# Projections of a two-layer attention and expert kernel on pairs of scaled 16-bit floats

## The chip, the cores and the metric

The kernel runs on one core of one Trainium2 chip. The metric is the device time of one execution in microseconds. The time given for a kernel is the median of several executions; the profile is of one further execution, whose own time is given beside its span.

## The reference

The reference is the trunk of a small encoder on x of 256 frames by 1024. Layer 0 mixes the frames by latent attention: x is projected to ranks (384 for queries, 256 for keys and values, 64 for a rotary key), the ranks are normalised, and then projected up to 8 heads. Layer 1 mixes them by attention over the 64 keys that a small indexer picks. Behind each mixer stands a layer of experts (PEER): a query picks, for each of 8 heads, the 16 best pairs of keys out of 128 x 128, that is 16 of 16384 experts. An expert is a row of w_down and a row of w_up.

```python
def _peer(x, w_q, sub_keys, w_down, w_up):
    q = (xt @ w_q).reshape(T, PEER_HEADS, 2, PEER_QDIM // 2)
    ...
    u = w_down[e_blk]
    a = jnp.einsum('td,ted->te', x_blk, u).astype(jnp.float32)
    hg = (jax.nn.gelu(a, approximate=False) * g_blk).astype(w_up.dtype)
    return jnp.einsum('te,ted->td', hg, w_up[e_blk]).astype(x_blk.dtype)

def reference(...):
    for i in range(DEPTH):
        m = _mla_mixer(...) if i % 2 == 0 else _dsa_mixer(...)
        x = _layernorm(DN_ALPHA * x + m, ln_gain[i, 0], ln_bias[i, 0])
        f = _peer(x, ...)
        x = _layernorm(DN_ALPHA * x + f, ln_gain[i, 1], ln_bias[i, 1])
    return x
```

The weights are normal with a spread of 1/32 for the projections from 1024, x is normal with spread 1, and the gains of the rank norms are about 8. Everything is in 32-bit floats.

## The kernel before, in words

The kernel doesn't gather experts (256 frames of 128 choices make 32768 choices of 16384 experts); it multiplies x by all 16384 down rows (product d, 128 blocks of 128 experts), applies the gelu, multiplies by a gate matrix that is zero where an expert was not chosen (built with the small product G from one-hot matrices), and multiplies by all up rows (product y). The array A in the arena holds gates and activations, 128 blocks by 256 frames.

Every projection works on pairs. A 32-bit operand is split in two: the high part is the value rounded to the type float32r by a copy on ScalarE, the low part is the value minus the high part, by VectorE. A product is three matmuls into one PSUM bank: high by high, high by low, low by high (`mm3`, `proj`, `rows`, all through `mm` at L277). `proj` makes a transposed result, with the weights stationary and x moving in 256 columns (24 matmuls a block); `rows` has x stationary and moves the weights in 512 columns (12 matmuls a block).

The class `Stream` holds the order of all weight blocks of the kernel, 128 x 1024 each, 604 in all: four raw buffers that SyncE fills by DMA (L101), and two rings of four places for the high and the low parts. `get` hands out the parts of one block and first fills the stream: blocks are split three ahead of the one that is taken, and loaded three ahead of that. `_split` makes the high part on ScalarE (L119) and the low part on VectorE (L123), or on GpSimd (L121) for one block in four while `share` says so. `_place` puts blocks whose parts are stationary 16 elements further along in the ring than blocks whose parts are moving (SKEW). The x of a stage is split once, into xh and xl.

The stages follow one another on TensorE: `mla` (0 to 105 us of the trace), `peer(0)` (to 878), `dsa` (to 1018), `peer(1)` (to the end). At the passage between two stages, `finish` interleaves the end of one product, the layer norm of the first half of the frames, and the start of the next product; the order there is written out by hand.

In `peer`, while TensorE works on d, VectorE works on the choice of experts in the background: `choose` is a generator that gives the cost of each of its steps in ns (1210 for a list of the 16 best of 128, 1160 for one of the pairs, and so on), and `spend` lets it run for an income of PACE after each block. So VectorE's order is: low part of a block, PACE worth of the choice, low part of the next. When the choice is done, the gates are made: for each group of four frames `prepare` builds one-hot matrices on VectorE (L1119), GpSimd (L1121) and ScalarE (L1125), `place` multiplies them (G, 8 matmuls of 128 columns, 16-bit) and writes the group into A. Two groups are placed for each pair of blocks of d.

`Norm` is a layer norm with its sums on VectorE (L351, with a sum written out beside the result), its squares on ScalarE (L359) and its power on GpSimd (L371). `first` is the first projection: it takes x and the first block in pieces, with a few idle matmuls at the start; one of its low parts is on GpSimd (L1227). `attention` works head by head: scores, exponentials on ScalarE (L578), transposes, outputs, which `split_ps` splits (L304, L305) for the output projection. In `finish` of the last stage, the output leaves by the queues of SyncE and ScalarE (L437).

Of the kernel before, what the change touches and what calls it, by code (L numbers as in the profile page):

```python
# [18 lines left out]
P = 128  # L19
T = 256  # L20
# [22 lines left out]
PACE = 1450  # L43
# [6 lines left out]
SKEW = 16  # L50
DSA_POOL = 3
MAGIC = 12582912.0


class Stream:
# [5 lines left out]
    def __init__(self, nc, raw, hi, lo):  # L61
        self.nc, self.raw, self.hi, self.lo = nc, raw, hi, lo
        self.dve = self.act = lambda emit: emit()
        self.blocks, self.ready = [], []
        self.at = []
# [5 lines left out]
    def add(self, src, w=D, moving=False):  # L71
        for i in range(src.shape[0]):
            self.blocks.append((src[i], w))
            self.at.append(self._place(0 if moving else SKEW))

    def _place(self, skew):

        if not self.at:
            return skew
        slot = (self.at[-1] // D + 1) % RING  # L80
        if slot and self.at[-1] + self.blocks[len(self.at) - 1][1] > slot * D + skew:
            slot = (slot + 1) % RING
        return slot * D + skew

    def _clear(self, n, first):

        a, b = self.at[n], self.at[n] + self.blocks[n][1]
        return all(self.at[m] + self.blocks[m][1] <= a or b <= self.at[m] for m in range(first, n))

    def parts(self, i):  # L90
        at = self.at[i]
        return [ring[:, at : at + self.blocks[i][1]] for ring in (self.hi, self.lo)]

    def _load(self, upto):
        while self.n_loaded <= min(upto, len(self.blocks) - 1):
            src, w = self.blocks[self.n_loaded]
# [15 lines left out]
    def _split(self, upto, pooled, first):  # L112
        nc = self.nc
        while self.n_split <= min(upto, len(self.blocks) - 1) and self._clear(self.n_split, first):
            w = self.blocks[self.n_split][1]
            self._load(self.n_split)
            raw = self.tiles[self.n_split][:, :w]
            hi, lo = self.parts(self.n_split)
            self.act(lambda: nc.scalar.copy(hi, raw))  # L119
            if pooled or self.share and (self.n_split - 1) % self.share == 0:  # L120
                nc.gpsimd.tensor_tensor(lo, raw, hi.bitcast(F32), op=ALU.subtract)  # L121
# [1220 lines left out]
```

## Time and profile before

| what | value |
|---|---|
| median of 3 runs | 1797.89 us (1797.75 to 1798.05) |
| the profiled execution's time | 1797.2 us |
| its span in the trace | 1795.4 us |
| granted TensorE clock | 0.999 |
| busy: PE, PEld, DVE, ACT, POOL | 1784.0, 1631.1, 1336.2, 1053.2, 406.2 us |
| read from HBM | 329.16 MB |

PE is TensorE's matmuls, PEld its loads of stationary operands, DVE VectorE, ACT ScalarE, POOL GpSimd, SP SyncE. A row of a group gives the line of the kernel, the engine and operation, what is written from what, the shape (partitions by elements, and type), and the count; then the busy time in us and the mean in ns of one, and the engine's idle time before them with what ended it. Matmuls overlap, so the mean of one is a latency; what one costs in a stream is the distance from start to start. In a timeline a row begins with its start and its length in us. In the chain of the execution that ended last, a piece is a stretch in which one engine went from one instruction to the next without a wait.

### The profile page before, as it was taken

Reading aid. Unit: us, or ns where it says so; the run is one execution under the profiler, and the core shown is the slowest. Engines: PE = TensorE matmul, PEld = TensorE weight load, DVE = VectorE, ACT = ScalarE, POOL = GpSimd, SP = SyncE. Lnnn points to the kernel's source line nnn. Section 1 sums busy time; section 2 is a strip of 40 time slices with the busy share of each in tenths; the row PEclk is TensorE's granted clock in tenths of the full one; section 3 lists DMA queues with packets and bytes.
Section 4 is the critical chain, followed back from the end, with each engine's and each line's share of the span. In section 5 each row is a group of like instructions: output and inputs, shape, how many; then the busy total and the mean of one; then the engine's idle time right before and its main releaser. Section 6 shows DMA issues by size and latency. Waiting matters only on the chain.

```text
span 1795.4 us, 32370 instructions
## 1 busy us (share of the span) xinstructions
PE 1784.0 (99%) x12495; PEld 1631.1 (91%) x12495; DVE 1336.2 (74%) x2319; ACT 1053.2 (59%) x1832; POOL 406.2 (23%) x288
## 2 busy tenths in 40 slices
PE   9999999999999999999999999999999999999998
PEld 8899999999998888888889899999999988888886
DVE  6688998888985555555688789997889865555555
ACT  6655545888864444444467554557888754444443
POOL 2012354555520000000023013544555400000000
PEclk9999999999999999999999999999999999999999
DMA  6555556444556565655646455565454476565553
GB/s 233 211 175 179 189 200 194 159 165 165 165 188 222 190 198 191 196 191 196 205 164 225 172 173 185 192 200 177 165 164 162 157 246 197 190 197 190 196 191 118
DMA packets 93468, 335.47 MB, mean 187 GB/s; under 512 B 10368, under 2 KB 11392, under 8 KB 93312
## 3 DMA queue, kind: packets, MB, share of 16 engines
q1 hardware_dynamic: 93024, 332.87, 56.0%
q8 instruction: 98, 1.61, 0.3%
q14 instruction: 58, 0.48, 0.1%
q10 hardware_dynamic: 288, 0.52, 0.1%
HBM read 329.16 MB, written 4.19 MB: 186 GB/s over the span
## 4 chain that ended last, share of the span: by engine, by line
PE 98%; DVE 1%; issue 0%; DMA 0%; ACT 0%; POOL 0%; SPq 0%; DVEq 0%; POOLq 0%; ACTq 0%
PE y L277 41%; PE d L277 39%; PE pq L277 4%; PE G L277 3%; PE q L277 3%; PE v L277 1%; PE qw L277 1%; PE s L277 1%; PE ps L277 1%; PE h L277 1%; PE qi L277 1%; PE o L277 1%; PE qn L277 0%; DMA raw<-in_mla_h 0%; PE pt L280 0%
## 5 line engine op out<-in xcount | busy, mean ns | idle before, releaser
L123 DVE TENSOR_TENSOR lo<-raw,hi 128x1024 fp32r<-128x1024 f32 (+1 forms) x556 | 747.5, 1346 | 289.5 <-ACT hi L119 288.0
L119 ACT CAST hi<-raw 128x1024 fp32r<-128x1024 f32 (+1 forms) x583 | 611.0, 1049 | 522.8 <-PE d L277 222.4
L277 PE MATMUL d<-xh,hi 128*128 128x256 f32 x2048 | 572.9, 280 | 0.0
L277 PE MATMUL d<-xh,lo 128*128 128x256 f32 x2048 | 566.8, 277 | 0.0
L277 PE MATMUL d<-xl,hi 128*128 128x256 f32 x2048 | 566.8, 277 | 0.0
L277 PEld LDWEIGHTS d<-xh,lo 128*128 128x128 f32 x2048 | 385.2, 188 | 0.0
L277 PEld LDWEIGHTS d<-xh,hi 128*128 128x128 f32 x2048 | 384.9, 188 | 0.0
L277 PEld LDWEIGHTS d<-xl,hi 128*128 128x128 f32 x2048 | 384.7, 188 | 0.0
L277 PE MATMUL y<-hi,xh 128*128 128x512 f32 x1088 | 337.8, 390 | 0.0
L277 PE MATMUL y<-lo,xh 128*128 128x512 f32 x1088 | 337.7, 389 | 0.0
L277 PE MATMUL y<-hi,xl 128*128 128x512 f32 x1088 | 337.2, 389 | 0.0
L1121 POOL TENSOR_TENSOR gate<-hot,gate 128x512 f16<-128x512 f16 x128 | 220.5, 1741 | 214.4 <-DVE hot L1119 214.4
L277 PEld LDWEIGHTS y<-lo,xh 128*128 128x128 f32 x1088 | 204.1, 188 | 42.8 <-DVE lo L123 0.3
L277 PEld LDWEIGHTS y<-hi,xl 128*128 128x128 f32 x1088 | 204.2, 188 | 42.4
L277 PEld LDWEIGHTS y<-hi,xh 128*128 128x128 f32 x1088 | 203.8, 188 | 41.9
L371 POOL TENSOR_TENSOR st<-st,mhalf 128x1 f32<-128x1 f32 x8 | 4.4, 550 | 802.1 <-DVE st L369 802.1
L1125 ACT ACTIVATE gate<-hot,rest 128x128 f16<-128x128 f16 x512 | 165.9, 411 | 1.1 <-DVE hot L1119 1.0
L1182 ACT CAST xh<-arena 128x512 fp32r<-128x512 f32 x128 | 79.7, 623 | 145.5 <-PE y L277 145.3
L1183 DVE TENSOR_TENSOR xl<-arena,xh 128x512 fp32r<-128x512 f32 x128 | 88.2, 692 | 72.7 <-ACT xh L1182 72.7
L121 POOL TENSOR_TENSOR lo<-raw,hi 128x1024 fp32r<-128x1024 f32 x27 | 65.2, 2414 | 218.4 <-ACT hi L119 213.1
L1119 DVE TENSOR_TENSOR hot<-iota,place 128x1024 f16<-128x1024 f16 x128 | 85.7, 709 | 32.3 <-PE G L277 32.2
L1043 POOL TENSOR_TENSOR arena<-arena 128x800 f32<-128x800 f16 x32 | 71.0, 2229 | 58.1 <-DVE arena L1040 58.1
(220 smaller groups left out, 1803.5 us busy)
## 6 DMA issues: line engine op xcount, KB each, us to landing
raw<-in_down SPq DMA_DIRECT2D x256, 512.0 KB, 3.3
raw<-in_up SPq DMA_DIRECT2D x256, 512.0 KB, 4.3
raw<-in_peer_q SPq DMA_DIRECT2D x24, 512.0 KB, 4.2
raw<-in_dsa_qk SPq DMA_DIRECT2D x16, 512.0 KB, 3.4
raw<-in_mla_w_o SPq DMA_DIRECT2D x8, 512.0 KB, 5.6
arena<-in_peer_q SPq DMA_DIRECT2D x8, 512.0 KB, 5.1
raw<-in_dsa_v SPq DMA_DIRECT2D x8, 512.0 KB, 4.4
raw<-in_dsa_w_o SPq DMA_DIRECT2D x8, 512.0 KB, 4.3
```

Source lines behind the costliest of these rows:

```text
L119: self.act(lambda: nc.scalar.copy(hi, raw))
L121: nc.gpsimd.tensor_tensor(lo, raw, hi.bitcast(F32), op=ALU.subtract)
L123: self.dve(lambda: nc.vector.tensor_tensor(lo, raw, hi.bitcast(F32), op=ALU.subtract))
L277: return pe(lambda: nc.tensor.matmul(o, l, r, start=start, stop=stop, skip_group_check=True))
L371: nc.gpsimd.tensor_tensor(st[:, 5:6], st[:, 4:5], mhalf, op=ALU.pow)
L1043: nc.gpsimd.tensor_tensor(o.rearrange("p k c -> p c k"), same, cell[t][:, h, :, None].to_broadcast([P, CELLS, TOPK]), op=ALU.mult)
L1119: nc.vector.tensor_tensor(hot, iota4[:, None].to_broadcast([P, 2, P, 4]), place16[:, :, None, four].to_broadcast([P, 2, P, 4]), op=ALU.is_ ...
L1121: nc.gpsimd.tensor_tensor(gate[:, 0], hot[:, 1].rearrange("p c j -> p j c"), gate16[:, four, None].to_broadcast([P, 4, P]), op=ALU.mult)
L1125: nc.scalar.mul(gate[:, 1, j, :], hot[:, 1, :, j], rest[:, t : t + 1])
L1182: nc.scalar.copy(hh, a)
L1183: nc.vector.tensor_tensor(al, a, hh.bitcast(F32), op=ALU.subtract)
```

## The change

The pairs become 16-bit floats (F16), with the value first scaled by a power of two: x by 2^12, the weights by 2^17, the normalised ranks by 2^9 and their weights by 2^16, the attention's outputs by 2^10 and the output weights by 2^17, A by 2^13 and the up rows by 2^14. The high part is a scaled copy on ScalarE to 16 bits; the low part is one operation on VectorE, value times scale minus high part, written in 16 bits. That operation also writes the sum of the low parts of each partition into a column of its own of an array `sums`. The scale is taken out where a result leaves PSUM (`unscale`, a scaled copy in the place of the copy; the gelu's scale; the rope tables, scaled on the host; the epsilon of the norms).

```diff
+class Split:
+    def high(self, o, src, unit, engine="act"):
+        nc, unit = self.nc, unit if self.short else 1.0
+        if engine == "act":
+            return nc.scalar.copy(o, src) if unit == 1.0 else nc.scalar.mul(o, src, unit)
...
+    def low(self, o, src, unit, hi, total=None):
+        nc = self.nc
+        if not self.short:
+            return nc.vector.tensor_tensor(o, src, hi.bitcast(F32), op=ALU.subtract)
+        return nc.vector.scalar_tensor_tensor(o, src, unit, hi, op0=ALU.mult, op1=ALU.subtract, accum_out=total)
...
+    half = F16 if short else F32R
...
-    xh = wide.tile([P, NC, T], F32R, tag="xh", name="xh")
-    xl = wide.tile([P, NC, T], F32R, tag="xl", name="xl")
+    xh = wide.tile([P, NC, T], half, tag="xh", name="xh")
+    xl = wide.tile([P, NC, T], half, tag="xl", name="xl")
```

The rings of `Stream` become pools of four tiles each, without the offset of SKEW and without the places that skip a part of the ring. Where GpSimd makes the low part, ScalarE scales the raw block in place first, and sums the low part later, when the stream is two blocks on:

```diff
+    def _pooled(self, i):
+        nc, short = self.nc, self.split.short
+        _, w, unit = self.blocks[i]
+        self._load(i)
+        raw = self.tiles[i][:, :w]
+        if short:
+            self.act(lambda: nc.scalar.mul(raw, raw, unit))
+        hi, lo = self.parts(i)
+        self.act(lambda: nc.scalar.copy(hi, raw))
+        self.ready.append((hi, lo))
+        nc.gpsimd.tensor_tensor(lo, raw, hi if short else hi.bitcast(F32), op=ALU.subtract)
+        if short:
+            self.late[i] = lo
+    def _add(self, i):
+        lo = self.late.pop(i, None)
+        if lo is not None:
+            total = self.split.total("both")
+            self.act(lambda: self.nc.scalar.activation(self.spare[:, : lo.shape[1]], lo, AF.Copy, accum_out=total))
+    def _split(self, upto, pooled):
+        while self.n_split <= min(upto, len(self.blocks) - 1):
+            i = self.n_split
+            if pooled or self.share and (i - 1) % self.share == 0:
+                self._pooled(i)
             else:
-                self.dve(lambda: nc.vector.tensor_tensor(lo, raw, hi.bitcast(F32), op=ALU.subtract))
-            self.ready.append((hi, lo))
+                self._high(i, self.act)
+                self._low(i, self.dve)
+            self._add(i - 2)
             self.n_split += 1
```

In `first`, the third low part goes from GpSimd to VectorE. PACE goes from 1450 to 1420. In `mla`, behind the load of x, GpSimd squares x and ScalarE sums the squares of each row:

```diff
-PACE = 1450
+PACE = 1420
...
+        if short:
+            for t in range(2):
+                nc.gpsimd.tensor_tensor(r2[t], x[t], x[t], op=ALU.mult)
+                nc.scalar.activation(r2[t], r2[t], AF.Copy, accum_out=sound_rows[:, t : t + 1])
...
-        pooled = x_low(2, "pool")
+        third = x_low(2)
```

At the end, between the two halves of the last norm, the columns of sums are tested: the square of each, summed over the partitions by a matmul with ones, must lie below 2^40, for most columns also at or above 64, and the sums of the rows of x at or above 4. The number of tests that hold is written to `sound`. The whole former program stands behind a branch that is taken when a test fails:

```diff
+    def judge(behind):
+        nc.gpsimd.tensor_tensor(cols, cols, cols, op=ALU.mult)
+        with tc.issue_after(behind.ins):
+            for i in range(n):
+                nc.tensor.matmul(p[:, i : i + 1], cols[:, i * P : (i + 1) * P], ones, start=True, stop=True)
+        nc.scalar.copy(least[:, :n], p[:, :n])
+        nc.gpsimd.tensor_scalar(fit[:, :n], least[:, :n], MOST, None, op0=ALU.is_lt)
+        nc.gpsimd.tensor_scalar(least[:, :both], least[:, :both], LEAST, None, op0=ALU.is_ge)
+        nc.gpsimd.tensor_tensor(fit[:, :both], fit[:, :both], least[:, :both], op=ALU.mult)
+        nc.gpsimd.tensor_scalar(fit[:, n:], sound_rows, ROW, None, op0=ALU.is_ge)
+        nc.tensor.matmul(q[0:1, :CHECKS], ones, fit, start=True, stop=True)
+        nc.scalar.activation(least[0:1, :], q[0:1, :CHECKS], AF.Copy, accum_out=fit[0:1, 0:1])
+        nc.scalar.copy(sound, fit[0:1, 0:1])
...
-        tile_trunk(tc, aps, o)
+        with tc.tile_pool(name="sound", bufs=1) as pool:
+            sound = pool.tile([1, 1], mybir.dt.int32, tag="sound", name="sound")
+            tile_trunk(tc, aps, o, True, sound)
+            count = nc.values_load(sound, min_val=0, max_val=P * CHECKS)
+            with tc.If(count < P * CHECKS):
+                tile_trunk(tc, aps, o, False)
```

More of the change, by code (lines that the diff above doesn't have):

```diff
@@ L69, in __init__, with add @@
         self.share = 0
-    def add(self, src, w=D, moving=False):
+        self.late = {}
+    def add(self, src, w=D, unit=W_UNIT):
         for i in range(src.shape[0]):
[L73 to L88, printed above, removed]
+            self.blocks.append((src[i], w, unit))
     def parts(self, i):
-        at = self.at[i]
-        return [ring[:, at : at + self.blocks[i][1]] for ring in (self.hi, self.lo)]
+        w = self.blocks[i][1]
+        return [self.rings.tile([P, D], self.dtype, tag=k, name=f"{k}{i}")[:, :w] for k in ("hi", "lo")]
     def _load(self, upto):
         while self.n_loaded <= min(upto, len(self.blocks) - 1):
-            src, w = self.blocks[self.n_loaded]
+            src, w, _ = self.blocks[self.n_loaded]
             if self.n_loaded in self.early:
@@ L303, in split_ps, with unscale @@
     def split_ps(hi, lo, p):
-        act(lambda: nc.scalar.copy(hi, p))
-        return dve(lambda: nc.vector.tensor_tensor(lo, p, hi.bitcast(F32), op=ALU.subtract))
+        total = split.total("most")
+        act(lambda: split.high(hi, p, O_UNIT))
+        return dve(lambda: split.low(lo, p, O_UNIT, hi, total))
+    def unscale(o, p, unit):
+        return nc.scalar.mul(o, p, 1.0 / unit) if short else nc.scalar.copy(o, p)
     def load_x(ar, src):
@@ L428, in finish @@
         if lead is None:
+            if sound is not None:
+                judge(last)
             n1.sums()
@@ L481, in finish @@
         do(1, "lh", 3)
+    def judge(behind):
+        assert not ws.late
+        n, both = (BOTH + MOSTLY) // P, BOTH // P
+        cols, p, q = split.cols, ps("sums"), ps("count")
+        fit = small.tile([P, CHECKS], F32, tag="fit", name="fit", bufs=1)
+        least = small.tile([P, CHECKS], F32, tag="least", name="least", bufs=1)
+        nc.gpsimd.tensor_tensor(cols, cols, cols, op=ALU.mult)
[10 more added lines that the diff above has]
+        nc.scalar.copy(sound, fit[0:1, 0:1])
     def operands(t, part, c, blk):
@@ L942, in peer @@
         last = li == DEPTH - 1
-        half = 64 * T
-        ar = Arena(arena, half)
+        middle = 64 * T
+        ar = Arena(arena, middle)
         qT, keys = ar.take(16, T), ar.take(16, NKEYS)
@@ L959, in peer @@
         scr = ar.ring(2, NKEYS)
-        qrow = [arena[:, half - (2 - t) * 512 : half - (1 - t) * 512] for t in range(2)]
+        qrow = [arena[:, middle - (2 - t) * 512 : middle - (1 - t) * 512] for t in range(2)]
         tail = s[0].rearrange("p a b -> p (a b)")
@@ L1181, in operand @@
                 hh, al = xh[:, slot, :], xl[:, slot, :]
-                nc.scalar.copy(hh, a)
-                nc.vector.tensor_tensor(al, a, hh.bitcast(F32), op=ALU.subtract)
+                total = split.total("most")
+                split.high(hh, a, A_UNIT)
+                split.low(al, a, A_UNIT, hh, total)
                 for j in range(2):
@@ L1262, in first @@
         passes(lo0, xh, 2, 3)
-        return pooled
+        return third
     mla()
```

183 lines of the change are left out of this document (106 added, 77 removed).

## The prediction

> **What bounds the kernel now.** First the head of the page, then the chain that ended last.
>
> ```profile
> span 1795.4 us, 32370 instructions
> PE 1784.0 (99%) x12495; PEld 1631.1 (91%) x12495; DVE 1336.2 (74%) x2319; ACT 1053.2 (59%) x1832; POOL 406.2 (23%) x288
> PE 98%; DVE 1%; issue 0%; DMA 0%; ACT 0%; POOL 0%; SPq 0%; DVEq 0%; POOLq 0%; ACTq 0%
> PE y L277 41%; PE d L277 39%; PE pq L277 4%; PE G L277 3%; PE q L277 3%; PE v L277 1%; PE qw L277 1%; PE s L277 1%; PE ps L277 1%; PE h L277 1%; PE qi L277 1%; PE o L277 1%; PE qn L277 0%; DMA raw<-in_mla_h 0%; PE pt L280 0%
> ```
>
> TensorE is on 98% of the chain, and two products, d (the experts' down rows) and y (their up rows, and the output projections), carry 80% of it. So the question is what one matmul costs when nothing holds it. The chain in order of time answers that, where one product runs without a break (start, us, what, count):
>
> ```profile
> 123.54 7.95 PE pq L277 x70
> 148.92 154.83 PE d L277 x1366
> 342.40 5.51 PE d L277 x48
> 347.91 0.93 PE G L277 x16
> 529.41 348.19 PE y L277 x1536
> 931.25 25.64 PE q L277 x216
> ```
>
> A 256-column matmul of d takes 154.83/1366 = 113.35 ns, a 512-column one of y 348.19/1536 = 226.69 ns (twice that), one of pq 113.6, one of q 118.7. Those rows are TensorE streaming; DVE, ACT and DMA are hidden behind it. How often each occurs is in the groups of TensorE by shape. Each of these rows has two sisters of the same count, because a product is high·high, high·low and low·high:
>
> ```profile
> L277 PE MATMUL d<-xh,hi 128*128 128x256 f32 x2048 | 572.9, 280 | 0.0
> L277 PE MATMUL y<-hi,xh 128*128 128x512 f32 x1088 | 337.8, 390 | 0.0
> L277 PE MATMUL pq<-xh,hi 128*128 128x256 f32 x192 | 53.7, 279 | 0.0
> L277 PE MATMUL q<-xh,hi 128*128 128x256 f32 x128 | 36.5, 285 | 0.0
> L277 PE MATMUL v<-hi,xh 128*128 128x512 f32 x40 | 12.5, 414 | 0.0
> L277 PE MATMUL qw<-hi,xh 128*128 128x512 f32 x32 | 8.8, 407 | 0.1
> ```
>
> The means of about 280 and 390 ns are latencies of overlapped matmuls; the spacing above is what counts.
>
> **The change on TensorE.** The number of matmuls and columns stays: three passes over two 16-bit parts instead of three over two rounded 32-bit parts. What can change is the price of a column. The trace has 16-bit matmuls of its own: G, 128 columns each. From the timeline:
>
> ```profile
> 321.79 1.09 PE L277 MATMUL G<-gate,hot 128*128 128x128 f16 x16
> 322.68 0.37 PE L277 MATMUL d<-xh,hi 128*128 128x256 f32 x1
> ```
>
> Sixteen G matmuls start within 322.68 - 321.79 = 0.89 us, 55.6 ns each, although each loads its own stationary operand. That is 0.434 ns a column; d and y pay 113.35/256 = 0.443. What decides is how much of the 55.6 ns is fixed per instruction. If none is, 256 columns take 111.2 ns and 512 take 222.4; that is the dear end. If a column takes 1/2.4 ns (an estimate: d's 113.35 ns and y's 226.69 ns are 17/16 of 256 and 512 columns at that price, and G's 128 columns at it are 53.3 ns, just under the 55.6), 2.3 ns are fixed, and 256 columns take 109.0, 512 take 215.7 ns. With nothing fixed but that price, 106.7 and 213.3 are the cheap end. I take the middle pair, as it alone gives G's own row and lies between the ends.
>
> A rule speaks against any gain: the Trainium skill, "TensorE: Matmul & The Clock Gate", section "Weight-path perf modes", says of fp8 that the array processes one element per cell per cycle regardless of element width. By it 16-bit and 32-bit parts would cost the same and the sum below would have no gain at all. No row here has the same shape in both types; that case is the first rival.
>
> The gains: d 6144 x (113.35 - 109.0) = 26.7 us; y 3264 x (226.69 - 215.7) = 35.9; pq 576 x (113.6 - 109.0) = 2.6; q 384 x (118.7 - 109.0) = 3.7; v and qw 216 x 11.0 = 2.4. Together 71.3 us. Smaller products (h, qi, qn and others) gain about 2 us more, which I leave in the range. With the dear end 2.2 ns x 7104 and 6.7 ns x 3480 go, 39 us; with the cheap end 2.3 x 7104 and 2.4 x 3480 come, 25 us.
>
> **What VectorE must now do in less time.** A block of d is 24 matmuls: 2.72 us before, 24 x 109.0 = 2.62 us after. In that time VectorE makes one low part, save on the blocks that GpSimd takes, and works off the choice of experts. Two windows (us; PE, PEld, DVE, ACT, POOL busy with counts; clock; DMA), VectorE's low parts in 150:200 and in 320:345, and timeline rows that show a subtraction against one with a sum:
>
> ```profile
> 145.00:200.00 55.00, 55.00 (x487) 55.00 (x486) 51.25 (x206) 27.28 (x33) 16.00 (x21) 1.00 0.59 185
> 1350.00:1420.00 70.00, 70.00 (x698) 69.61 (x697) 64.34 (x77) 57.37 (x154) 37.82 (x22) 1.00 0.48 163
> L123 DVE TENSOR_TENSOR lo<-raw,hi 128x1024 fp32r<-128x1024 f32 x14 | 17.1, 1222 | 1.3 <-ACT hi L119 1.2
> L123 DVE TENSOR_TENSOR lo<-raw,hi 128x1024 fp32r<-128x1024 f32 x8 | 13.2, 1653 | 3.2 <-ACT hi L119 3.2
> 6.18 1.29 DVE L1227 TENSOR_TENSOR xl<-arena,xh 128x512 fp32r<-128x512 f32 x2
> 1787.32 0.69 DVE L351 SCALAR_TENSOR_TENSOR arena<-arena,y 128x512 f32<-128x512 f32 x1
> 1787.93 0.08 DVE L351 DVE_READ_ACCUMULATOR arena<-arena,y 128x1 f32 x1
> 1788.00 0.69 DVE L351 SCALAR_TENSOR_TENSOR arena<-arena,y 128x512 f32<-128x512 f32 x1
> ```
>
> The scaled subtraction runs 0.69 us for 512 elements, like the plain one (two in 1.29 us, so 0.60 from start to start); the read of its sum brings the next start to 0.68. So a low part costs up to 0.08 us more; I take 0.05, between that and nothing. In 145:200 VectorE is busy 51.25/55 x 2.72 = 2.53 us a block; 14 low parts (17.1 us) in some 18 blocks of the inner 50 us are 0.93 of that, the choice is 1.60. PACE falls from 1450 to 1420, which takes 2% of the 1.60 off; with the added sum on three blocks in four that makes 2.54 of 2.62 us, 97%. Near the end of d a pair of blocks and two G groups take 5.51 + 0.93 = 6.44 us, of which VectorE is busy 64.34/70 x 6.44 = 5.92; after, 6.02 of 48 x 109.0 ns + 0.93 = 6.16 us, 98%. It fits, barely. The high and low parts of a block are begun three blocks ahead, so a jitter of some us is absorbed; I take 3 us lost over both layers, with 0 and the second rival's 29 as ends. The choice takes about 98,000 units of cost in all (32 x 1210 for the first lists, then pairs and experts), so it ends 1 to 2 blocks later; the G groups still go two to a pair, and TensorE's work does not change.
>
> A rule bears on this, too: the Trainium skill, "SBUF — State Buffer", section "SBUF: two separate sides", says that a VectorE operation with two SBUF inputs and a GpSimd operation reading SBUF exclude each other, whichever starts first holding the shared ports. The trace agrees in size: a low part takes 1222 ns in 150:200 and 1653 ns in 320:345, where GpSimd works on the gates. By it, faster matmuls leave both engines less time for the same exclusive spans, which is the second rival.
>
> **ScalarE, GpSimd, the start.** The high part becomes a scaled copy, which I cost like the cast. A block whose low part GpSimd makes now has two more ScalarE instructions, a scaling before and a sum after:
>
> ```profile
> L119 ACT CAST hi<-raw 128x1024 fp32r<-128x1024 f32 x582 | 610.5, 1050 | 522.8 <-PE d L277 222.4 <-PE y L277 208.7 <-PE pq L277 30.3
> L359 ACT ACTIVATE arena<-arena,st 128x1024 f32<-128x1024 f32 x8 | 9.3, 1162 | 25.6 <-DVE st L354 25.6
> L121 POOL TENSOR_TENSOR lo<-raw,hi 128x1024 fp32r<-128x1024 f32 x27 | 65.2, 2414 | 218.4 <-ACT hi L119 213.1 <-PE pt L280 5.3
> 20.00:60.00 40.00, 39.91 (x296) 37.88 (x295) 30.36 (x70) 31.00 (x64) 6.84 (x7) 1.00 0.66 229
> 880.00:970.00 90.00, 89.74 (x651) 81.24 (x650) 73.51 (x151) 56.08 (x98) 20.34 (x14) 1.00 0.59 203
> ```
>
> That is 27 x (1.05 + 1.16) = 60 us of ScalarE, most of it in the choice, where ScalarE is busy 27.28 of 55 us and the block is begun three blocks (7.8 us) ahead: free. Transfers, 4.3 us each to landing (below) into four buffers, have 10.5 us for the round. If that cover were gone, each would delay its block by its 2.2 us. A few fall into the second layer's attention (ScalarE 56.08 of 90 us), and the row test of x adds two squares on GpSimd and two sums on ScalarE (2 x 1.16) behind the load of x in the first layer's attention (ScalarE 31.00 of 40 us). ScalarE is in order, so an exponential or a copy queued behind them waits. I take 3 us for both; nothing to 2.3 + 4 x 2.2 = 11 us. At the start, one low part moves from GpSimd to VectorE ahead of the halves of the first block's low part: 0.6 us by the row above; I take 0.5.
>
> **The end.** The test multiplies the sums on GpSimd, runs seven one-column matmuls behind the last of y, then alternates ScalarE, five small GpSimd steps, one matmul and ScalarE, and then all engines read the count and branch past the former program.
>
> ```profile
> 1787.57 0.39 PE L277 MATMUL y<-hi,xl 128*128 128x512 f32 x1
> 1792.58 0.34 ACTq L437 DMA_DIRECT2D out_y<-arena  x1
> L732 POOL TENSOR_TENSOR arena<-arena,mhalf 128x2 f32<-128x2 f32 x2 | 1.4, 706 | 10.3 <-DVE arena L731 10.3
> L277 PE MATMUL ms<-ones,arena 128*128 128x1 f32 x8 | 1.0, 230 | 0.0
> raw<-in_up SPq DMA_DIRECT2D x256, 512.0 KB, 4.3
> ```
>
> The last matmul starts at 1787.57, and the last output leaves at 1792.58 of 1795.4. The test needs some 7 x 0.11 + 0.4 + 4 x 0.5 + 0.3 + 0.5 + 0.4 = 4.4 us after the last matmul (estimates from the short rows), so the count is there as the output leaves. The last norm's square waits on ScalarE behind the test's first copy, its power on GpSimd behind the test's steps. No row shows a register load or a far branch. Nothing can be gained here, since work is only added; nothing is lost if all fits under the output's landing (2.8 us); two reads as slow as a block's transfer (4.3 each) cost 8.6. I take 4 us, the middle.
>
> **Sum.** 1795.4 - 71.3 + 3 + 3 + 0.5 + 4 = 1734.6 us of span. The profiled execution took 1797.2, 1.8 above its span, and the median of the three runs, 1797.89, is 0.7 above that: **1737 us**. Its own bounds are 1712 (cheap columns) and 1776 (dear ones).
>
> **Rivals.** *No gain per column.* If 16-bit parts stream at 113.35 and 226.7 ns, only the added 10.5 us remain: 1797.9 + 10.5 = 1808, slower. It decides once 15% or less of the 71.3 us comes, that is, from 225.1 ns for 512 columns on. For it: G's 0.434 ns a column is near d's 0.443. Against: the part of 55.6 ns that must be fixed. 6%.
>
> *VectorE becomes the bound in d.* If contention and the sums make a low part 0.2 us longer than I say, or if it cannot use the shorter block at all, d keeps its old pace: 26.7 + 2.6 - 3 = 26 us back, 1763; between, about 1750. For it: 97 and 98%. Against: three blocks of lead. 16%.
>
> *The placing of the buffers.* The change drops the offset of 16 elements between stationary and moving blocks. q's 118.7 ns against d's 113.35 shows that the same matmul has a slower form. If all 16-bit matmuls of 256 columns took 5.3 ns more, 7104 x 5.3 = 38 us would go: 1775. Nothing shows that the offset is its cause. 6%.
>
> *The test fails, and the former program runs behind it*: 1737 + 1798 = 3535. The weights have a spread of 1/32 x 2^17 = 4096 after scaling, x and the norms' outputs 4096, the ranks (gain 8) 8 x 2^9 = 4096, the attention's output 8 x 2^10 = 8192; a half float ends at 65504, eight spreads away at the nearest, and residuals of some units over 1024 columns are far above 64. 3%.
>
> My forecast has the other 69%. A measurement tells 0.2%, about 4 us, from no change. Faster: 69 + 16 + 6 = 0.91; of the first rival one part in six ends within the 4 us, so same 0.01, slower 0.08. The range 1720 to 1768 takes in the forecast's unknown costs and the second rival.
>
> **What would show it.** In the changed profile a free run of d at 109 ns and of y at 216 ns a matmul; G unchanged; low parts of about 1.25 us with a read of the sum behind each; no idle TensorE in d; the span's end a few us behind the output. A y spacing above 225 ns, gaps in d that end on a low part, or a second half of the trace would show me wrong.

## The result, and the profile after

The changed kernel takes 1737.18 us (median of 4 runs, 1734.94 to 1740.81) against 1797.97 (1797.75 to 1798.24) for the kernel before on the same chip: a ratio of 0.9664, with a 95% interval of 0.9647 to 0.968. The prediction was 1737, in a range of 1720 to 1768. The profiled execution took 1734.94 us, its span is 1733.1: 62.3 us less than before. The head of the page and its chain:

```profile
span 1733.1 us, 33286 instructions
PE 1705.0 (98%) x12511; PEld 1192.4 (69%) x12511; DVE 1345.5 (78%) x3063; ACT 1104.7 (64%) x1916; POOL 406.0 (23%) x295
PE 88%; DVE 6%; ACT 2%; DMA 2%; issue 2%; POOL 1%; SPq 0%; DVEq 0%; ACTq 0%; POOLq 0%
```

There are 16 more matmuls (the test's), as many on PEld, and PEld is busy 1192 us instead of 1631: the load of a stationary operand takes 98 ns on the mean in 16 bits and took 188 in 32. In the kernel before, the loads were hidden in y: PEld was busy 171 of the 207 us of the window 593:800. In d it was busy all 55.00 us of the window 145:200, so that window alone can't say whether columns or loads set d's old price; but y, with loads to spare, paid the same 0.443 ns a column. TensorE's share of the chain falls from 98% to 88%; what came into it is VectorE, ScalarE, DMA and "issue": faster columns leave the other engines less time to stay hidden. Now the pieces of the chain in order of time (start, us, what, count), the counterpart of the fence that carried the prediction:

```profile
121.18 7.64 PE pq L337 x70
145.71 83.64 PE d L337 x766
313.52 5.24 PE d L337 x48
319.65 5.24 PE d L337 x48
508.89 331.52 PE y L337 x1536
919.36 5.24 PE q L337 x48
```

A matmul of d now costs 83.64/766 = 109.2 ns, one of y 331.52/1536 = 215.8, one of pq 109.1, one of q 109.2; before they were 113.35, 226.69, 113.6 and 118.7. A pair of blocks of d with its two G groups takes 319.65 - 313.52 = 6.13 us, which is 48 x 109.2 ns + 16 x 55.6 ns to the digit.

The ledger of the two profiled executions, from the first matmul of a stage to the first of the next one (or to the end of the span), in us. The forecast's terms are put to the stages in which they belong:

| stage | before | after | difference | forecast |
|---|---|---|---|---|
| start | 6.30 | 6.31 | 0.0 | in the next row |
| both attentions (without qw) | 211.81 | 209.93 | -1.9 | q 3.7, v 1.3, w_o's y 2.1, against 3 + 0.5: -3.6 |
| qw and pq, both layers | 105.49 | 101.85 | -3.6 | 2.6 + 1.1: -3.7 |
| d to the first G, both layers | 341.04 | 343.32 | +2.3 | |
| d with G, both layers | 425.74 | 392.54 | -33.2 | both d rows: -26.7 + 3 = -23.7 |
| y, both layers | 697.21 | 663.90 | -33.3 | 3072 x 10.99: -33.8 |
| last matmul to the end | 7.86 | 15.30 | +7.4 | +4 |
| sum | 1795.4 | 1733.1 | -62.3 | -60.8 |

The two rows of d belong together: the choice ended two blocks later, so 1536 matmuls run ahead of the first G instead of 1488. Together they give 30.9 us. So y, pq and qw came out as forecast, d gave 7 us more, the attentions 2 us less, and the end cost 3 us more. The profiled execution is the fastest of the four, 2.2 us below their median.

The groups that the steps touched, with busy time, mean ns of one, and the engine's idle time before them:

```profile
L96 DVE SCALAR_TENSOR_TENSOR lo<-raw,hi 128x1024 f16<-128x1024 f32 (+1 forms) x571 | 760.4, 1334 | 256.1 <-ACT hi L87 254.7
L337 PE MATMUL d<-xh,lo 128*128 128x256 f16 x2048 | 558.3, 273 | 3.8 <-POOL lo L165 2.1
```

VectorE's low part is still the largest thing beside TensorE, and TensorE now stands 3.8 us for low parts of d, 2.1 of them for GpSimd's. The end, from the timeline (start, length):

```profile
1717.85 0.38 PE L337 MATMUL y<-hi,xl 128*128 128x512 f16 x1
1718.06 1.62 PE L559 MATMUL sums<-ones,sums 128*128 128x1 f32 x14
...
1722.67 0.17 ACT L566 ACTIVATE least<-count 1x9 f32<-1x9 f32 x1 [2.08 <-PE count L565]
...
1722.96 0.19 ACT L567 CAST sound<-fit 1x1 int32<-1x1 f32 x1
1722.97 0.34 ACTq L503 DMA_DIRECT2D out_y<-arena  x1
```

The output leaves 1722.97 - 1717.85 = 5.1 us after the last matmul of y, and before it left 5.0 us after: the test delays the last norm by 0.1 us. It is what stands behind that is new; from the rows of the lines of the load and the branch (duration min/median/max in ns, first and last start):

```profile
L1436 PEldq TENSOR_LOAD <-sound x1: 682/682/682, 1723.2 to 1723.2; - x1
L1437 ACTq COMPARE_BRANCH  x1: 54/54/54, 1723.9 to 1723.9; - x1
L1437 PEldq COMPARE_BRANCH  x1: 3929/3929/3929, 1724.0 to 1724.0; - x1
L1437 ACTq EVENT_SEMAPHORE  x1: 17/17/17, 1728.0 to 1728.0; - x1
L1437 SPq EVENT_SEMAPHORE  x8: 17/17/17, 1728.3 to 1731.7; - x8
```

The load of the count takes 0.7 us. Then every engine needs about 4 us from its branch, at 1723.9 to 1724.2, to its next instruction, at 1728.0 to 1728.3; TensorE's queue shows it as a branch of 3929 ns. SyncE's last semaphore of the branch is at 1731.7, and the span ends 10.1 us behind the issue of the last output, where it was 2.8.

### The profile page after: what moved, and what is told of

Its sections match the earlier page's. It is cut to its first block, busy times and chain, and to the rows that moved or that the text cites. A ratio compares the mean times of both kernels' runs of the same rounds, so it can differ in the third digit from the quotient of the medians.

```text
span 1733.1 us, 33286 instructions
## 1 busy us (share of the span) xinstructions
PE 1705.0 (98%) x12511; PEld 1192.4 (69%) x12511; DVE 1345.5 (78%) x3063; ACT 1104.7 (64%) x1916; POOL 406.0 (23%) x295
## 4 chain that ended last, share of the span: by engine, by line
PE 88%; DVE 6%; ACT 2%; DMA 2%; issue 2%; POOL 1%; SPq 0%; DVEq 0%; ACTq 0%; POOLq 0%
PE y L337 40%; PE d L337 35%; PE pq L337 3%; PE G L337 3%; DVE lo L96 2%; PE v L337 1%; PE ps L337 1%; PE h L337 1%; PE q L337 1%; ACT hi L87 1%; PE s L337 1%; PE qw L337 0%; DMA raw<-in_down 0%; PE o L337 0%; PE qn L337 0%
## 5 line engine op out<-in xcount | busy, mean ns | idle before, releaser
L96 DVE SCALAR_TENSOR_TENSOR lo<-raw,hi 128x1024 f16<-128x1024 f32 (+1 forms) x571 | 760.4, 1334 | 256.1 <-ACT hi L87 254.7
L87 ACT ACTIVATE hi<-raw 128x1024 f16<-128x1024 f32 (+1 forms) x570 | 597.6, 1051 | 345.6 <-PE y L337 188.8
L337 PE MATMUL d<-xh,lo 128*128 128x256 f16 x2048 | 558.3, 273 | 3.8 <-POOL lo L165 2.1
L337 PE MATMUL d<-xh,hi 128*128 128x256 f16 x2048 | 558.2, 273 | 0.2 <-ACT hi L87 0.2
L337 PE MATMUL d<-xl,hi 128*128 128x256 f16 x2048 | 558.2, 273 | 0.0
L337 PEld LDWEIGHTS <-hi 128*128 128x128 f16 x5016 | 488.0, 98 | 59.8 <-issue 3.0
L337 PE MATMUL y<-lo,xh 128*128 128x512 f16 x1088 | 326.2, 379 | 0.0
L337 PE MATMUL y<-hi,xl 128*128 128x512 f16 x1088 | 325.9, 379 | 0.0
L337 PE MATMUL y<-hi,xh 128*128 128x512 f16 x1088 | 325.5, 379 | 0.0
L337 PEld LDWEIGHTS <-lo 128*128 128x128 f16 x2508 | 245.4, 98 | 35.2 <-DVE lo L96 3.9
L337 PEld LDWEIGHTS <-xl 128*128 128x128 f16 x1160 | 113.4, 98 | 138.6 <-DVE xl L96 2.1
```

Of the source, the lines that this page charges most:

```text
L87: return nc.scalar.copy(o, src) if unit == 1.0 else nc.scalar.mul(o, src, unit)
L96: return nc.vector.scalar_tensor_tensor(o, src, unit, hi, op0=ALU.mult, op1=ALU.subtract, accum_out=total)
L337: return pe(lambda: nc.tensor.matmul(o, l, r, start=start, stop=stop, skip_group_check=True))
```

## The experiments

Ratios are against runs of the kernel before on the same chip, with 95% intervals. A part of them was chosen because only the sum of the prediction is confirmed by the time: its steps could be wrong and cancel.

**The branch alone.** The test stays, the count is not read and nothing stands behind it.

```diff
             tile_trunk(tc, aps, o, True, sound)
-            count = nc.values_load(sound, min_val=0, max_val=P * CHECKS)
-            with tc.If(count < P * CHECKS):
-                tile_trunk(tc, aps, o, False)
```

> The changed kernel without the read of the count, the branch and the former program behind it; the test itself stays and its count is unused. Theory A (the end is long because each engine's jump over the former program costs some 4 us and SyncE stops once more): the stretch from the last matmul of y to the end falls from 15.3 us to about 8, as before the change (7.9), the rest of the trace stays, time about 1737.2 - 7 = 1730. Rival B (the test's steps hold the last norm): the stretch stays above 11 us and the gain is under 4 us.

1732.19 us (1729.46 to 1733.92, 5 runs), ratio 0.9637 (0.9623 to 0.965). In the trace the end falls from 15.3 to 8.0 us after the last matmul, against 7.86 in the kernel before. So the test itself costs 0.2 us there, and load and branch 7.3: the end is theory A's, and rival B is refuted. The medians differ by 5.0 us, and the time is 2 us above A's 1730; the changed kernel's own runs spread over 6 us, so the trace is the better measure.

**A near branch.** The load and the branch stay, but five short instructions take the place of the former program.

```diff
             with tc.If(count < P * CHECKS):
-                tile_trunk(tc, aps, o, False)
+                nc.vector.memset(near, 0.0)
+                nc.tensor.matmul(sums, near[:, 0:1], near, start=True, stop=True)
+                nc.scalar.copy(near, sums)
+                nc.gpsimd.tensor_scalar(near, near, 1.0, None, op0=ALU.mult)
+                nc.sync.dma_start(o[0:1, 0:4], near)
```

> The changed kernel with five short instructions, one for each engine, in the place of the former program behind the branch; the branch isn't taken to them. Theory A (the 4 us come from jumping far, past some 16000 instructions that were not fetched): TensorE's branch falls from 3.9 us to under 1, and the end by 4 to 6 us, time about 1732. Rival B (a branch costs 4 us wherever it leads): the branch stays at 3.9 us and the time at 1737.

1733.22 us (1731.29 to 1735.62, 5 runs), ratio 0.964 (0.9626 to 0.9653); the end is 9.7 us. The same two instructions in this kernel, and the issue of its last output from the timeline:

```profile
L1436 PEldq TENSOR_LOAD <-sound x1: 678/678/678, 1728.7 to 1728.7; - x1
L1437 PEldq COMPARE_BRANCH  x1: 228/228/228, 1729.6 to 1729.6; - x1
1729.74 0.34 ACTq L503 DMA_DIRECT2D out_y<-arena  x1
```

The load is the same, the branch takes 0.23 us instead of 3.93, as theory A said, and the end falls by 15.3 - 9.7 = 5.6 us: that is what the former program behind the branch costs, by its length or by what else stands behind it (SyncE has eight semaphores there, one behind the near branch). The other 9.7 - 8.0 = 1.7 us are not the bare price of a load and a branch: in this trace the last output is issued behind the branch, 6.4 us after the last matmul instead of 5.1, and that is most of it.

The two pages count different numbers of transfers of instructions on their queues (transfers, MB, share). The first two rows are the changed kernel's, the others the near branch's:

```profile
q8 instruction: 100, 1.64, 0.4%
q14 instruction: 74, 0.61, 0.1%
q8 instruction: 98, 1.61, 0.4%
q14 instruction: 65, 0.53, 0.1%
```

The 11 more all lie behind the far branch: by the trace's records of single transfers, five begin between 1724.9 and 1725.6, while the engines stand, five between 1728.6 and 1729.2, and one at 1732.4. So instructions are fetched there. The Trainium skill, "Runtime: NRT & Kernel Launch", section "Instruction fetch mechanics", says that a taken branch to a target outside the window of instructions held makes the engine wait until it is fetched. These two traces agree with it, and give the price; but a transfer itself takes 0.3 to 1.0 us, and what fills the rest of the 4 us is not shown.

**All sums left out.** No sum behind a low part, none of GpSimd's and ScalarE's row sums, no test, no branch.

```diff
     def total(self, kind):
-        if not self.short:
-            return None
+        return None
...
-        if lo is not None:
+        if False:
             total = self.split.total("both")
...
-        if short:
+        if False:
             for t in range(2):
...
-            tile_trunk(tc, aps, o, True, sound)
...
+        tile_trunk(tc, aps, o, True)
```

> The changed kernel without any of the range test: no sums beside the low parts, no sums of GpSimd's low parts on ScalarE, no row sums of x, no test, no branch. Theory A (VectorE at 97 to 98% loses TensorE's time in the choice of experts only by its bare work; a sum is 0.05 us): beyond the branch's 7 us it brings 2 to 4 us, most of it in the choice, where the d before the first G takes 170.7 and 172.7 us, and some in the two attentions; about 1727. Rival B (the sums are what stops TensorE in the choice): the choice falls to 169 us in both layers, and the time to 1722 or below. Rival C (the sums cost nothing): 1730, as without the branch.

1723.23 us (1721.53 to 1725.37, 5 runs), ratio 0.9588 (0.9575 to 0.9601): 9 us less than without the branch alone. In the traces of the two, 2.1 us come in the first attention, 2.0 in the second, 1.1 and 1.2 in d ahead of G, and nothing in y. So the sums and the test cost some 14 us, of which the branch is 5 (medians) to 7 (trace), and the sums cost most where the attentions are: there the gain against the kernel before is 8.3 us without sums, where the columns alone were forecast to give 7.1, and 1.9 with them. Both attentions are shorter here than in each of the nine 16-bit traces with sums, by 1.2 us or more. The 1.2 us in d are not shown to be the sums' work: the second layer's d ahead of G takes 175.4 us here and 169.3 to 176.6 in the others. None of the three theories had it so: the time lies between A's and B's, the choice did not fall to B's 169 us, and the gain is not, as A had it, mostly in the choice.

**The former program in the new frame.** The same file, run with 32-bit parts: the new rings without the offset, no test.

```diff
-            tile_trunk(tc, aps, o, True, sound)
...
+        tile_trunk(tc, aps, o, False)
```

> The new structure (rings as pools of tiles without the offset, PACE 1420, the third low part of the first projection on VectorE, iota in the arena) with the former two rounded 32-bit parts, no test and no branch. Theory A (the gain is the price of a column in 16 bits): d streams at 113.3 ns and y at 226.7 again, 1795 to 1803. Rival B (the offset and the places in the rings made the slow form of 117 to 119 ns that 14% of d's matmuls had): that form is gone or everywhere, and the time is 1785 or below, or 1815 or above.

1838.51 us (1837.97 to 1838.96, 4 runs), ratio 1.0227 (1.0212 to 1.0243): 41 us slower than the kernel before, with the same arithmetic. Two pieces of its chain:

```profile
152.05 166.79 PE d L337 x1390
548.71 348.19 PE y L337 x1536
```

d costs 166.79/1390 = 120.0 ns a matmul, y 226.7 as before. That is rival B's second case: the slower form is everywhere in d. So something in the new frame changes the price of a 32-bit matmul of d, and by more than the 16-bit parts gain on one; the next runs ask whether it is the placing. y, untouched by it, compares the types in one frame: 226.7 ns here, 215.8 in the 16-bit kernel without its branch.

**The offset, put back.** Three kernels give blocks whose parts are stationary a start further along in their tiles (which blocks these are is said where they are added to the stream, not shown here). The first has 32-bit parts, 16 elements (64 bytes), and tiles that are 64 bytes longer:

```diff
-        return [self.rings.tile([P, D], self.dtype, tag=k, name=f"{k}{i}")[:, :w] for k in ("hi", "lo")]
+        a = 0 if self.moving[i] else 16
+        return [self.rings.tile([P, D + 16], self.dtype, tag=k, name=f"{k}{i}")[:, a : a + w] for k in ("hi", "lo")]
```

> The new structure with the former 32-bit parts, no test and no branch, as in the run of the old parts, but with the blocks whose parts are stationary 64 bytes further along in their tiles, as the former rings had them. Theory A (the 120 ns that d's matmuls took without the offset are a collision of stationary and moving addresses, which the offset avoids): d and pq stream at 113.3 ns again and the time is 1797 to 1803. Rival B (the pools of tiles or their place in memory cost it, not the offset): d stays at 120 ns and the time at 1838.

1830.45 us (1830.28 to 1830.69, 4 runs), ratio 1.0181 (1.0165 to 1.0196). Neither theory's number:

```profile
151.40 161.88 PE d L342 x1390
540.20 354.80 PE y L342 x1536
```

d is 116.5 ns on the mean, and single blocks are at 113.5 to 114.1 or at 118 to 120; y has risen to 231.0. Tiles that are 64 bytes longer also move each other on by 64 bytes, which may undo the offset for some of them. The next one has tiles 128 bytes longer:

```diff
-        return [self.rings.tile([P, D + 16], self.dtype, tag=k, name=f"{k}{i}")[:, a : a + w] for k in ("hi", "lo")]
+        return [self.rings.tile([P, D + 32], self.dtype, tag=k, name=f"{k}{i}")[:, a : a + w] for k in ("hi", "lo")]
```

> The former 32-bit parts in the new structure with the offset again, but with tiles longer by 128 bytes instead of 64, so that every stationary block begins at an odd multiple of 64 bytes and every moving one at an even multiple; in the run before, tiles longer by 64 bytes made that alternate, and d's blocks took 113 and 120 ns in turn. Theory A (a 32-bit matmul costs one sixteenth more when stationary and moving parts begin alike in 128 bytes): all of d at 113.3 ns, y at 226.7, 1797 to 1803. Rival B (the alternation has another cause, such as the order of the buffers): d still mixes 113 and 120 ns, 1825 or more.

1812.12 us (1812.09 to 1812.38, 4 runs), ratio 1.0081 (1.0065 to 1.0096):

```profile
150.18 157.64 PE d L342 x1390
529.86 353.73 PE y L342 x1536
```

d is back at 157.64/1390 = 113.4, the kernel before's own price; y, where x is stationary and the block moves, stays dear at 230.3. So the theory held for d where it streams and not for y, nor for the time, and which distance between two 32-bit operands is harmless is not settled by these three. The third is the 16-bit kernel without its branch, with the same 64 bytes (32 elements):

```diff
-        return [self.rings.tile([P, D], self.dtype, tag=k, name=f"{k}{i}")[:, :w] for k in ("hi", "lo")]
+        a = 0 if self.moving[i] else 32
+        return [self.rings.tile([P, D + 32], self.dtype, tag=k, name=f"{k}{i}")[:, a : a + w] for k in ("hi", "lo")]
```

> The changed kernel without the branch, with the stationary blocks 64 bytes further along in their tiles. Theory A (16-bit parts don't have that collision): d stays at 109.2 ns and y at 215.8, the time at 1730 to 1734 like the kernel without the branch. Rival B (16-bit matmuls have a collision of their own that this placing happens to meet or leave): d's spacing moves by 4 ns or more.

1730.72 us (1730.07 to 1731.08, 4 runs), ratio 0.9626 (0.9611 to 0.964), against 1732.19 without the offset:

```profile
145.61 83.64 PE d L342 x766
508.68 331.52 PE y L342 x1536
```

109.2 and 215.8, the prices of the changed kernel to the digit. With 16-bit parts this placing does nothing.

**No low parts on GpSimd.** POOLED = 0: VectorE makes every low part, and ScalarE's scaling and sum for GpSimd's blocks go.

```diff
-POOLED = 4
+POOLED = 0
```

> The changed kernel with POOLED = 0: in the choice of experts GpSimd makes no low parts, so some 11 more of them a layer go to VectorE (about 1.2 us each), and ScalarE loses two instructions for each. Theory A (VectorE is the bound of the choice, with nothing to spare): 11 x 1.2 = 13 us a layer, less the 1.5 us that are free, come on top, 10 to 25 us in all, 1747 to 1762, with the d before the first G above 176 us. Rival B (VectorE still has slack there, the short stalls come from late transfers): within 4 us of 1737.

1735.31 us (1732.88 to 1736.77, 4 runs), ratio 0.9655 (0.9641 to 0.967): no dearer, where theory A, of an engine at its limit, wanted 13 us a layer; the time is rival B's. The window of the choice (us, then busy times with counts of PE, PEld, DVE, ACT, POOL; clock; DMA) and VectorE's low parts in 150:200, in the changed kernel:

```profile
143.00:200.00 57.00, 57.00 (x524) 51.18 (x523) 52.47 (x223) 37.54 (x48) 15.45 (x21) 1.00 0.51 184
L96 DVE SCALAR_TENSOR_TENSOR lo<-raw,hi 128x1024 f16<-128x1024 f32 x13 | 17.4, 1342 | 0.0
```

and without GpSimd's low parts:

```profile
143.00:200.00 57.00, 56.55 (x519) 50.53 (x518) 54.70 (x220) 29.31 (x34) 4.24 (x16) 1.00 0.51 175
L96 DVE SCALAR_TENSOR_TENSOR lo<-raw,hi 128x1024 f16<-128x1024 f32 x17 | 20.6, 1212 | 0.0
```

VectorE makes 17 low parts instead of 13 in 3.2 us more, not in 5.4. The mean of 1342 ns hides why: in the changed kernel (duration min/median/max) one of the 13 is the whole difference, and the timeline shows it behind a low part of GpSimd's:

```profile
L96 DVE SCALAR_TENSOR_TENSOR lo<-raw,hi x13: 1205/1206/2869, 151.4 to 195.7; 128x1024 f16<-128x1024 f32 x13
183.33 2.13 POOL L165 TENSOR_TENSOR lo<-raw,hi 128x1024 f16<-128x1024 f32 x1 [7.74 <-ACT hi L163]
183.68 2.87 DVE L96 SCALAR_TENSOR_TENSOR lo<-raw,hi 128x1024 f16<-128x1024 f32 x1
```

VectorE's started 0.35 us after GpSimd's and ended 1.1 us after it; the others, two of which VectorE had begun before GpSimd's, took 1.21 to 1.31 us as without GpSimd. So in this window GpSimd puts 2.87 - 1.21 = 1.7 us back on VectorE of the 4 x 1.2 that it takes off. Busy rises only from 92 to 96%. This is the exclusion that the prediction named beside its 1222 and 1653 ns (the Trainium skill, "SBUF — State Buffer", section "SBUF: two separate sides"): the one that starts first holds the other up, and with one side taken away no low part of the window is over 1.31 us. It frees little on TensorE: d up to the first G takes 172.0 us in both layers, where the changed kernel has 170.7 and 172.7.

**The stall in the second layer.** Before the first G of the second layer the changed kernel's TensorE stands longer than in the first. A stretch of the timeline:

```profile
1123.48 2.21 POOL L1118 TENSOR_TENSOR arena<-arena 128x64 f32<-128x64 f32 x11
...
1123.53 4.63 DVE L1115 TENSOR_TENSOR arena<-arena 128x40 f32<-128x40 f32 x14
...
1125.66 2.11 POOL L165 TENSOR_TENSOR lo<-raw,hi 128x1024 f16<-128x1024 f32 x1
...
1126.03 0.27 PE L337 MATMUL d<-xl,hi 128*128 128x256 f16 x1
...
1127.83 0.28 PE L337 MATMUL d<-xh,lo 128*128 128x256 f16 x1 [1.52 <-POOL lo L165]
```

GpSimd's low part is queued behind its share of the choice's pair sums (L1118, beside VectorE's at L1115), starts at 1125.66 and takes 2.11 us; TensorE reaches the block's low part before it is there and waits 1.5 us. An income of 1390 a block in place of 1420, and one block of spare time in place of two between the choice and the gates:

```diff
-PACE = 1420
+PACE = 1390
...
-            yield 2 * PACE
+            yield 1 * PACE
```

> The changed kernel with PACE 1390 in place of 1420 and one spare block instead of two behind the choice, so that the choice still ends in time. Theory A (the stalls of 1.6 and 3.6 us before the first G are VectorE falling behind): VectorE's work a block falls by about 0.03 us, the stalls shrink by half, 1733 to 1736. Rival B (the stalls are single collisions with GpSimd in the experts' part, not a lack of VectorE time): they stay, 1736 to 1739.

1733.84 us (1731.03 to 1734.45, 5 runs), ratio 0.9639 (0.9626 to 0.9652). The second layer's d up to the first G takes 169.3 us instead of 172.7. The first layer's is 171.5 instead of 170.7, and the second attention is 127.5 instead of 125.5, where this edit changes nothing. So the time lies in theory A's range, but only one layer's stall shrank, and this run doesn't part A from rival B. This edit together with the one before, on GpSimd's low parts:

> The changed kernel with PACE 1390, one spare block, and no low parts on GpSimd in the choice: the two edits of the choice that were each no slower, together. Theory A (VectorE is close to its limit but not over it, and GpSimd's low parts cost VectorE as much as they take off it): the d before the first G falls under 171 us in both layers, 1731 to 1734. Rival B (each edit moved the stalls by chance): 1735 to 1738.

1732.19 us (1729.56 to 1734.65, 5 runs), ratio 0.9634 (0.962 to 0.9647); d up to the first G takes 171.1 us in both layers, just above theory A's 171, and the time is A's. It beats the kernel before and, in the medians, the changed kernel, by 5 us.

**The former program, taken.** The condition holds always, so both programs run. In the trace no engine branches at L1437, and SyncE alone reads the count: the run shows what the former program takes behind the new one, not a branch that is decided as it runs.

```diff
-            with tc.If(count < P * CHECKS):
+            with tc.If(count < P * CHECKS + 1):
```

> The changed kernel with the branch always taken, so that the former program runs behind the new one, as it would if a test failed. Theory A (the price of a failed test is one run of the former program): 1737 + 1795 = 3530 to 3540. Rival B (the second program starts cold, with its instructions to be fetched and its weights not loaded ahead): 3545 or more.

3569.41 us (one run). The window behind the first program's end, columns as above, and the first long piece of d in it:

```profile
1740.00:3567.00 1827.00, 1817.87 (x12470) 1668.22 (x12469) 1336.46 (x2309) 1048.06 (x1825) 393.14 (x276) 1.00 0.53 182
1882.82 166.79 PE d L337 x1390
```

TensorE is busy 1817.9 of the 1827 us. The second program adds 3569.4 - 1737.2 = 1832 us: not the 1798 of the kernel before, for it is the former program in the new frame (1838.5), at 166.79/1390 = 120.0 ns a matmul of d; and the first program, which jumps nowhere here, ends some us sooner. The time is in rival B's range, but not for B's reason: the 120 ns alone make some 40 us of it, and no cold start of that size shows.

**The changed kernel again**, on the chip of the run with tiles 128 bytes longer:

> The changed kernel itself once more, beside the others on the same chip. Theory A (the two edits of the choice are worth the 3 to 5 us that the runs showed): 1735 to 1739. Rival B (the changed kernel's own spread covers them): 1731 to 1735.

1737.04 us (1734.05 to 1739.47, 5 runs), ratio 0.9663 (0.965 to 0.9676). In its trace y takes the same to 0.1 us and the end 15.1 us; d up to the first G of the second layer takes 174.8 us instead of 172.7. In the other traces that leave the choice alone it reaches 176.6, and the second attention takes 123 to 127.5 us: in these two stages lies most of the spread of 5 to 6 us that the kernel before, with 0.5 us, did not have. The lower pace with no GpSimd parts lies below it: the intervals of their ratios, 0.962 to 0.9647 and 0.965 to 0.9676, do not meet, and that of the changed kernel's first runs begins where the former ends. They come from different chips and the gap is small, and the two profiled executions are alike (1734.65 and 1734.94 us), so the 5 us between the medians is a likely gain rather than a certain one.

## Why the prediction was right, step by step

**The price of a column: right.** 109.0 and 215.7 ns were forecast out of G's 55.6 and the 1/2.4 ns worked out from d and y; 109.2 and 215.8 came. y and the small products in qw and pq, 37.5 us, gave 36.9. The first rival, no gain per column, is refuted not only by the time: in the same frame, y takes 215.8 ns in 16 bits and 226.7 in 32. (The times there, 1732.19 and 1838.51 us, differ by more because d is at 120 ns in the second.) The rule of the Trainium skill on element width ("TensorE: Matmul & The Clock Gate", section "Weight-path perf modes"), which speaks of fp8 and would have it so, does not hold for these 32-bit parts in this case: at the best placing seen, a 32-bit matmul takes 1.04 (113.35 to 109.2) to 1.05 (226.7 to 215.8) of the 16-bit one's time, and more at a worse one.

**d: mis-sized, on the good side.** 6144 x (113.35 - 109.2) = 25.5 us is the term, forecast as 26.7. What was left out is that the stretch with the G groups was dearer than the free stream says: two layers of 1584 matmuls of d and 512 of G make 2 x (1584 x 113.35 + 512 x 55.6 ns) = 416.0 us, and took 425.7, which is 9.7 more. After, 2 x (1536 x 109.2 + 512 x 55.6 ns) = 392.4, and it takes 392.5. With the 4.2 us of the next point taken off, 25.5 + 9.7 gives the 30.9 that came, to 0.1. The prediction quoted 5.51 us for 48 matmuls there, 114.8 ns each, and passed over it. The timelines show where over half of it lies (the first row is the kernel before, behind the row at 322.68 that the prediction shows; the others are the changed kernel):

```profile
322.88 0.28 PE L277 MATMUL d<-xl,hi 128*128 128x256 f32 x1
324.73 1.06 PE L337 MATMUL G<-gate,hot 128*128 128x128 f16 x16
325.62 0.27 PE L337 MATMUL d<-xh,hi 128*128 128x256 f16 x1
325.73 0.27 PE L337 MATMUL d<-xl,hi 128*128 128x256 f16 x1
```

From the first matmul of d behind G to the second it is 0.20 us in the kernel before, at every G group, and 0.11 us after: 64 x 0.09 = 5.8 us. The rest is in single blocks beside G at 117 to 118 ns a matmul. Whether the passage costs this because the type changes, or because a 32-bit load (188 ns) isn't hidden behind G's short matmuls, was not tried.

**VectorE: right in size, wrong in its reading.** Ahead of the first G, 1536 x 109.2 = 167.7 us is the floor; 170.7 and 172.7 are 2.9 and 4.9 over it, where before 1488 x 113.35 = 168.7 stood under 170.5 twice, 1.9 over. (Some 1.2 of the 1.9 are the small products ps and gT, which stand there before and after.) So waits cost 4.2 us more in this profile (3 forecast) and 6.4 in the repeat's. But "97 and 98%, it fits, barely" made too much of it: with four more low parts in the window VectorE got through at 96%. The second rival, VectorE as the bound, would have needed d at its old pace. Of the waits of d for low parts, 2.1 us are for GpSimd's and 1.6 for VectorE's; at least the first are a matter of order (GpSimd's long low part behind other work) and not of VectorE's sum of work.

**The attentions: mis-sized.** 3.5 us were set for the sums and scalings there and at the start, where nothing of them shows (6.31 us against 6.30); without sums and test the same stages take 4.1 us less than without the branch alone, and 6.4 less than in the changed kernel's trace. The upper end that was kept, 11, holds it. Which of the added instructions costs it was not taken apart.

**The end: mis-sized.** 4 us were taken as the middle of 0 and 8.6; 7.4 came. The test before the branch is hidden as forecast (8.0 against 7.86); the price is the far branch, 5.6 of it, which no row before showed. These two errors and the one of d cancel in the sum: -60.8 forecast, -62.3 in the span. That the median then is 1737.18 for a forecast of 1737 is luck; the gain on y, more than half of the sum, is not. All three lay within the bounds given, d's inside those of the cheap columns (6144 x 6.65 = 40.9 us), but for a reason that the prediction did not have. Two of its own signs of being wrong showed in part: TensorE stands 3.8 us for low parts in d, and the span ends 10 us behind the output, not a few.

**The placing: the rival's mechanism is real, its object is not.** "Nothing shows that the offset is its cause" was said of q's slower form. For 32-bit parts placing does make a d matmul 120 ns instead of 113.4, which the tile lengths show. For 16-bit parts, the ones that the change uses, the one shift that was run (64 bytes) changes nothing, so the rival's 38 us did not come. The offset could be dropped for no price only because the parts went to 16 bits in the same change.

**The test failing** did not happen. Its price was given as 1798 and is 1832 in the one run that was made, for the former program behind the branch has lost its offset.

Still open: why the second attention takes 121 to 127.5 us in traces of kernels that differ little there, what a 32-bit operand's address must avoid (in the four placings of 32-bit parts that were run, neither d nor y went below 113.3 and 226.7 ns on the mean, but a cheaper one isn't excluded), and whether 16-bit parts have a placing of their own to avoid, of which two were run.

## What to carry to other kernels

Put the start-to-start distance of a streaming matmul against its columns before anything else: if it is above what a small 16-bit product in the same trace leads one to expect, the operand type or its address may be what is paid for; where TensorE had no other wait, as in y, the gain came back whole (33.3 us of 33.8). A guard that is never taken still costs: keep what stands behind its branch short, or try the branch away from the end, which was not done here. An engine at 97% in a profile isn't yet a bound; take its helper away and see whether the time moves. And look at the shortest and the longest behind a mean: one collision can look like a slower instruction.

## What the runs showed of the hardware

A branch past a program of some 12,000 matmuls held every engine about 4 us, and instructions were transferred meanwhile; one past five instructions took 0.23 us on TensorE. Reading the count took 0.53 to 0.69 us on each engine. In the far case SyncE's semaphores behind the branch stretched over 3.4 us more. A low part on VectorE of 1.21 us took 2.87 when it began 0.35 us after one on GpSimd. A 256-column matmul on 32-bit parts took 113.4, 116.5 or 120.0 ns, and a 512-column one 226.7 to 231.0, by where the operands lie: between 116.5 and 113.4, and between 231.0 and 230.3, only the tiles' length differs. 16-bit ones took 109.2 and 215.8 in both placings that were run. Behind a group of 16-bit matmuls the first 32-bit one took 0.20 us to the next, a 16-bit one 0.11.
